# Loading, masks and hi/lo copies at the beginning of a hybrid encoder layer, rearranged

## The chip, the cores and the metric

The kernel runs on one core of a Trainium2 chip. Its engines are TensorE (PE; its weight loads are listed as PEld), VectorE (DVE), ScalarE (ACT), GpSimd (POOL) and SyncE (SP, which here only issues transfers). Each works through its own queue in order, and waits on semaphores for the others. The metric is the device time of one execution in microseconds (us).

## The reference

One layer of an encoder, 1024 tokens of width 1024, in float32:

```
u = rmsnorm(x, norm_mix_pre)
proj = u @ w_in                # columns: qa ka va ga | za (gate, 32) | qs ks vs
o_a = gated linear attention, both directions, from qa ka va za; then norm * silu(ga)
o_s = windowed attention (|i-j| <= 128) of 8 query and 2 key heads, with bias and sink
x = x + rmsnorm(concat(o_a, o_s) @ w_out, norm_mix_post)
x = x + rmsnorm(relu(rmsnorm(x, norm_mlp_pre) @ w_up)^2 @ w_down, norm_mlp_post)

rmsnorm(x, g) = x * rsqrt(mean(x*x) + 1e-6) * g
```

## The kernel before

Products are made of float32r parts: each operand is split into a hi part (a rounding copy) and a lo part (the rest, by a subtraction), and hi·hi, lo·hi and hi·lo are summed in PSUM. This is `dense_part`, 24 matmuls for 8 slices of the inner dimension.

The beginning is written out by the string `START`, one token a step. `x3` loads tile 3 of x (128 tokens, 512 KB) on SP's queue. `p3` (`norm_x`) makes u of that tile, transposed: ScalarE squares the tile with a sum per token (L292) and adds epsilon (L176); GpSimd raises to the power -1/2 (L181, called the power below); VectorE scales the tile by that and by the norm weights (`gb`, L294); TensorE transposes it in eight 128x128 blocks into two PSUM banks (`pxt`, L171); of each bank a hi copy goes to `uth` (by ScalarE, L93, or VectorE, L95) and then a lo copy to `utl` (VectorE, L302). `HALF_X` names the engine of each of the 16 hi copies, `a` for ScalarE and `v` for VectorE. There are two such banks in all, so a tile's transposes wait for the lo copies of the tile before.

`f` fetches a weight tile (512 KB, 128 columns of w_in) into `raw`; VectorE makes its hi part `wh`, GpSimd its lo part `wl` (L196). There are two `raw` buffers. `v01` is the v projection (vs) of tiles 0 and 1 from the first weight tile, `k02` the k projection (ks) of tiles 0 to 3 from the second, both into `pkv`; `k22`, `v11`, `v22` are the rest of both. `W` loads the gate's columns, `z02` and `z22` project them (`pz`), `gates`, `misc`, `bias` and `spread` set up small things. After `START` comes `gates(0)` with the first matmul into `pg`, and the long list `ORDER`.

`gb`, the norm weights in all 128 partitions, is made by `load_gb`: a 4 KB row is loaded, and two matmuls with a row of ones spread it over the partitions, from where VectorE copies it. `set_misc` builds `wdiag` and `mask_lt`, used later by the linear attention, on GpSimd.

Instructions stand in the program in this order, but a scheduler places them in the queue of each engine; the order of a queue is then fixed.

Of the kernel before, what the change touches and what calls it, by code (L numbers as in the profile page):

```python
# [13 lines left out]
F32 = mybir.dt.float32  # L14
# [3 lines left out]
ALU = mybir.AluOpType  # L18
# [38 lines left out]
 'pvo': 'lg'}  # L57

EVAC = {'vf': 'v', 'vt': 'v', 'kt': 'v', 'th': 'v'}
HALF_X = "avvvaavavvvvavvv"  # L60
W_HI = "vvaavv"
W_LO = "gggggg"

START = (
        "gb x0 x1 f p0 x2 x3 p1 p2 f v01 p3 W x4 x5 x6 x7 p4 p5 k02 gates p6 p7 bias k22 v11 z02 v22 f f misc "
        "z22 spread "
)

# [10 lines left out]
def hybrid_layer(tc, x, g_mix_pre, w_in, w_gu_f, b_g_f, w_gu_b, b_g_b, gla_norm, sink, rel_bias, w_out,  # L81
                 g_mix_post, g_mlp_pre, w_up, w_down, g_mlp_post, onehot, relmask, out):
    nc = tc.nc

    def Q(name):
        return getattr(nc, QUEUE[name])

    def E(c):
        return dict(v=nc.vector, g=nc.gpsimd)[c]

    def C(c, dst, src):
        if c == "a":
            nc.scalar.copy(dst, src)  # L93
        else:
            E(c).tensor_copy(dst, src)  # L95

    order = ORDER.split()
    with ExitStack() as ctx:
# [5 lines left out]
        def bank(tag, name="bk"):  # L104
            return ps.tile([128, 512], F32, tag=tag, bufs=BUFS[tag], name=name)

        def slot(tag, kb, dt, name, bufs=1):
            t = sb.tile([128, int(kb * KB)], dt, tag=tag, bufs=bufs, name=name)

            def cut(off, n, *shape):  # L110
                ap = t[:, int(round(off * KB)):int(round(off * KB)) + n]
                if len(shape) == 2:
                    ap = ap.rearrange("p (a b) -> p a b", a=shape[0])
                return ap

            def cut3(off, a, b):
                return cut(off, a * b, a, b)

            cut.three = cut3
            return cut  # L120
# [4 lines left out]
        wdiag = cst(0.5, 128)  # L125
        mask_t = sb.tile([128, 128], I32, name="mask_lt")
        mask_lt = mask_t[:, :]
        so = [1.0]

        def small(n):  # L130
            ap = cst(so[0], n)
            so[0] += n / KB
            assert so[0] <= 3.25 + 1e-9, so
            return ap
# [6 lines left out]
        dsc = small(32).rearrange("p (h n) -> p h n", h=4)  # L141
# [9 lines left out]
        def tiny(n=8, ring="misc"):  # L151
            r = rings[ring]
            r[1] += 1
            return r[0][r[1] % len(r[0])][:, 0:n]

        nc.scalar.preload_act_table_set("natural_log_exp_and_others")
        nc.gpsimd.memset(ident, 1.0)
        nc.gpsimd.affine_select(out=ident, in_=ident, pattern=[[1, 128]], base=0, channel_multiplier=-1,
                                compare_op=ALU.is_equal, fill=0.0)
        nc.vector.memset(mhalf, -0.5)  # L160
        nc.vector.memset(epsc, EPS)
        orow = wdiag[0:1]
        nc.vector.memset(orow, 1.0)
        nc.vector.memset(sgn[0:64, 0:1], 1.0 / 16)
        nc.vector.memset(sgn[64:128, 0:1], -1.0 / 16)
        nc.vector.memset(sgn[0:64, 1:2], -1.0 / 16)
# [61 lines left out]
            return p  # L228


        e0 = slot("G0", 16, F32, "e0")
        e1 = slot("G1", 16, F32, "e1")
        e2 = slot("G2", 16, F32, "e2")
        e2x = slot("GX", 4, F32, "e2x")
# [27 lines left out]
            return r  # L262


        gb = e0(12, 1024)
        xts = [e0(4 * t, 1024) for t in range(3)] + [s2(4 * t, 1024) for t in range(4)]
        xt = []

        def load_x(t):
            xt.append(xts[t % 7])  # L270
            nc.sync.dma_start(xt[t], x[0, t * 128:(t + 1) * 128, :])

        def load_gb():
            gr = e1(8, 1024)[0:1]
            nc.sync.dma_start(gr, g_mix_pre)
            for c in range(2):
                p = bank("ga", "pgb")
                nc.tensor.matmul(p, lhsT=orow, rhs=gr[:, c * 512:c * 512 + 512], start=True, stop=True)
                C("v", gb[:, c * 512:c * 512 + 512], p)

        zw = e4.three(0, 8, 64)

# [6 lines left out]
        def norm_x(t):  # L289
            xn = e1(4 * (t % 2), 1024)  # L290
            ss = tiny(1)
            nc.scalar.activation(xn, xt[t], AF.Square, scale=1.0 / 32, accum_out=ss)  # L292
            r = rstd_of(ss)
            nc.vector.scalar_tensor_tensor(out=xn, in0=xt[t], scalar=r, in1=gb, op0=ALU.mult, op1=ALU.mult)  # L294
            for k4 in range(2):
                p = bank("tr", "pxt")
                transpose4(p, [xn[:, (k4 * 4 + j) * 128:(k4 * 4 + j + 1) * 128] for j in range(4)])
                p3 = p.rearrange("p (a b) -> p a b", a=4)
                h_ = uth[t // 4][:, k4 * 4:k4 * 4 + 4, (t % 4) * 128:(t % 4 + 1) * 128]
                l_ = utl[t // 4][:, k4 * 4:k4 * 4 + 4, (t % 4) * 128:(t % 4 + 1) * 128]  # L300
                C(HALF_X[2 * t + k4], h_, p3)
                nc.vector.tensor_sub(l_, p3, h_)  # L302
# [5 lines left out]
        bias = s2.three(0, 8, 384)  # L308

        def set_misc():  # L310
            nc.gpsimd.memset(wdiag, 1.0)
            nc.gpsimd.affine_select(out=wdiag, in_=wdiag, pattern=[[1, 128]], base=0, channel_multiplier=-1,
                                    compare_op=ALU.not_equal, fill=2.0)
            nc.gpsimd.memset(mask_lt, 1)
            nc.gpsimd.affine_select(out=mask_lt, in_=mask_lt, pattern=[[1, 128]], base=0, channel_multiplier=-1,
                                    compare_op=ALU.is_gt, fill=0)
            nc.gpsimd.memset(dsc, 0.0)
            Q("misc").dma_start(gnh, gla_norm.rearrange("a p -> p a"))
            sk = tiny(8)
            Q("misc").dma_start(sk, sink.broadcast_to([128, 8]))  # L320
            nc.vector.tensor_scalar(nsink, sk, -1.0, None, op0=ALU.mult)
# [106 lines left out]
        for tok in START.split():  # L428
            k, a = tok[0], tok[1:]
            if k == "x":  # L430
                load_x(int(a))
            elif k == "p":
                norm_x(int(a))
            elif k in "zvk":
                q0, n = int(a[0]), int(a[1])
                if k == "z":
                    z_part(q0, n)
                else:
                    kv_part({"v": "vs", "k": "ks"}[k], q0, n)
            else:  # L440
                {"gb": load_gb, "W": load_zw, "f": fetch_next, "misc": set_misc, "gates": set_gates,
                 "bias": set_bias, "spread": spread_bias}[tok]()

        scm = e2(12.5, 264)
# [6 lines left out]
        W = W2.rearrange("p (c j) -> p c j", j=66)  # L451
# [640 lines left out]
        for q, (p, j) in enumerate(seq):  # L1092
# [32 lines left out]
            if (p, j) in ((1, NP - 1), (2, NP - 1)):  # L1125
                u0 = 4 * (p - 1)
                t = slot(("U2", "U3")[p - 1], 16, F32, "wd")
# [7 lines left out]
        for (r, c), tags in (((1, 0), ("S0", "G0")), ((1, 1), ("G1", "U0")), ((0, 1), ("U1",))):  # L1135
            for h, tag in enumerate(tags):
                t = slot(tag, 16, F32, "wd")
# [79 lines left out]
        for n, (i, u) in enumerate(steps):  # L1217
            p, _, _, banks = plan[i]
            sd, td = double(2 * n), double(2 * n + 1)
            for t in range(4):  # L1220
                for c in range(2):
                    for m, (a, b) in enumerate(((0, 0), (0, 1), (1, 0))):
                        nc.tensor.matmul(banks[t], lhsT=sd[a][:, c * 512 + t * 128:c * 512 + t * 128 + 128],  # L1223
                                         rhs=td[b][:, c * 512:c * 512 + 512],
                                         start=p in (1, 2, 3, 5) and u == 0 and c == 0 and m == 0,
                                         stop=u == 7 and c == 1 and m == 2, skip_group_check=True)
# [81 lines left out]
```

## Time and profile before

| | us |
|---|---|
| median of 3 runs | 1085.55 (1084.59 to 1087.48) |
| the profiled execution | 1088.56 |
| its span, first to last instruction | 1086.8 |
| TensorE busy | 1048.9 |
| VectorE busy | 744.0 |
| ScalarE busy | 525.5 |
| GpSimd busy | 161.4 |

Times in the trace count from the start of the span. The profiled execution's own time is 1.8 us above its span. Matmuls are pipelined, so TensorE's busy time includes some waiting inside it; the weight loads (PEld) show its pace.

### The profile page before, as it was taken

What the parts mean: (1) busy time and instruction counts of PE and PEld (TensorE: products, weight loads), DVE (VectorE), ACT (ScalarE), POOL (GpSimd) and SP (SyncE); (2) the same over time, 40 slices, a digit from 0 to 9 for tenths busy, and PEclk for the clock granted to TensorE, in tenths of its full rate; (3) what the DMA queues carried; (4) which work ended last, traced back from release to release, by engine and by line L of the source; (5) the groups of instructions that cost most, each with busy time, mean ns of one, the idle gap of its engine ahead of it and who ended that gap; (6) DMA issues with size and microseconds to landing.
All of it is one profiled execution on the core that took longest, in us unless ns stands there. A gap on an engine that the chain in (4) does not pass through costs nothing.

```text
span 1086.8 us, 13683 instructions
## 1 busy us (share of the span) xinstructions
PE 1048.9 (97%) x4950; PEld 858.0 (79%) x4950; DVE 744.0 (68%) x1165; ACT 525.5 (48%) x890; POOL 161.4 (15%) x246
## 2 busy tenths in 40 slices
PE   7999999999997999989999999999999999999996
PEld 5787788888885878768888888888778888888885
DVE  7659458799887767798665666564479764547564
ACT  5565324424766444466555555554444334345342
POOL 4211012111211111111221212112100000004002
PEclk9999999999998999999999999999999999999999
DMA  7355443613666432546563544537982333345522
GB/s 227 111 159 173 131 115 84 143 40 93 190 171 162 122 121 84 160 152 207 177 191 116 177 143 148 172 119 238 392 325 97 98 97 97 116 136 193 194 97 97
DMA packets 138805, 164.82 MB, mean 152 GB/s; under 512 B 17473, under 2 KB 94273, under 8 KB 138738
## 3 DMA queue, kind: packets, MB, share of 16 engines
q1 hardware_dynamic: 108626, 108.36, 32.2%
q0 software_dynamic: 22560, 37.76, 11.6%
q10 hardware_dynamic: 7552, 17.83, 5.1%
q8 instruction: 39, 0.64, 0.2%
q14 instruction: 28, 0.23, 0.1%
HBM read 111.47 MB, written 52.45 MB: 151 GB/s over the span
## 4 chain that ended last, share of the span: by engine, by line
PE 81%; DVE 9%; ACT 3%; issue 3%; DMA 3%; POOL 1%; SPq 0%; ACTq 0%; DVEq 0%; POOLq 0%
PE pa L994 16%; PE pa L1223 14%; PE pin L222 11%; PE pc L994 8%; PE pb L1223 6%; PE pc L1223 6%; PE pm L810 4%; PE pb L994 4%; PE pkv L222 2%; PE ppt L171 1%; PE pm L815 1%; PE pl L545 1%; DMA wd<-in_w_down_dram 1%; PE pkv L692 1%; PE pl L546 1%
## 5 line engine op out<-in xcount | busy, mean ns | idle before, releaser
L1223 PE MATMUL pa<-r 128*128 128x512 f32 x768 | 175.1, 389 | 0.8 <-DVE r L1163 0.8
L1223 PEld LDWEIGHTS pa<-r 128*128 128x128 f32 x768 | 144.0, 188 | 31.4 <-DVE r L1163 1.6
L1162 DVE TENSOR_TENSOR r<-ra,r 128x1024 fp32r<-128x1024 f32 x56 | 68.5, 1223 | 106.7 <-ACT r L1160 105.3
L1160 ACT CAST r<-ra 128x1024 fp32r<-128x1024 f32 x56 | 58.9, 1053 | 165.9 <-PE pa L1223 94.1
L994 PE MATMUL pa<-th,r 128*128 128x512 f32 x384 | 102.3, 389 | 0.7 <-ACT sn L1009 0.7
L994 PEld LDWEIGHTS pa<-th,r 128*128 128x128 f32 x384 | 72.0, 188 | 16.0 <-ACT sn L1009 1.1
L222 PE MATMUL pin<-uth,wh 128*128 128x512 f32 x256 | 70.9, 400 | 0.0
L1223 PE MATMUL pb<-r 128*128 128x512 f32 x288 | 69.7, 390 | 0.0
L222 PE MATMUL pin<-uth,wl 128*128 128x512 f32 x256 | 69.4, 396 | 0.0
L1223 PE MATMUL pc<-r 128*128 128x512 f32 x288 | 69.2, 389 | 0.0
L810 PE MATMUL pm<-wo,b 128*128 128x512 f32 x256 | 67.5, 403 | 1.5 <-ACT b L802 1.5
L222 PE MATMUL pin<-utl,wh 128*128 128x512 f32 x256 | 66.9, 392 | 0.0
L1163 DVE TENSOR_TENSOR r<-wd,r 128x1024 fp32r<-128x1024 f32 x52 | 63.4, 1219 | 3.8 <-ACT r L1161 3.8
L1223 PEld LDWEIGHTS pb<-r 128*128 128x128 f32 x288 | 53.9, 188 | 11.9 <-DVE r L1163 0.7
L1223 PEld LDWEIGHTS pc<-r 128*128 128x128 f32 x288 | 54.1, 188 | 11.2
L180 POOL TENSOR_SCALAR cst<-cst 128x1 f32<-128x1 f32 x16 | 12.1, 754 | 323.6 <-ACT wd L1185 288.7
L1068 DVE TENSOR_TENSOR r<-su,r 128x1024 fp32r<-128x1024 f32 x32 | 39.0, 1220 | 28.9 <-ACT r L1067 28.9
L1161 ACT CAST r<-wd 128x1024 fp32r<-128x1024 f32 x52 | 54.6, 1050 | 5.4 <-DMA wd<-in_w_down_dram 5.4
L810 PEld LDWEIGHTS pm<-wo,b 128*128 128x128 f32 x256 | 47.5, 192 | 11.3 <-ACT b L802 2.4
L222 PEld LDWEIGHTS pin<-utl,wh 128*128 128x128 f32 x256 | 47.8, 188 | 9.7
L1002 ACT ACTIVATE ar<-ar 128x512 f32<-128x512 f32 x42 | 26.6, 632 | 56.3 <-DVE ar L1013 56.3
L222 PEld LDWEIGHTS pin<-uth,wl 128*128 128x128 f32 x256 | 47.0, 188 | 8.4
(282 smaller groups left out, 2136.3 us busy)
## 6 DMA issues: line engine op xcount, KB each, us to landing
ra<-hss SPq DMA_DIRECT2D x32, 512.0 KB, 3.6
wd<-in_w_down_dram SPq DMA_DIRECT2D x28, 512.0 KB, 9.3
hss<-ar POOLq DMA_DIRECT2D x54, 256.0 KB, 5.0
ra<-hsx SPq DMA_DIRECT2D x24, 512.0 KB, 3.8
hsx<-ar POOLq DMA_DIRECT2D x47, 256.0 KB, 2.9
ra<-in_w_up_dram SPq DMA_DIRECT2D x16, 512.0 KB, 4.1
rb<-in_w_up_dram SPq DMA_DIRECT2D x16, 512.0 KB, 5.9
raw<-in_w_in_dram SPq DMA_DIRECT2D x14, 512.0 KB, 4.6
```

What stands on the lines that cost most here:

```text
L171: nc.tensor.transpose(dst_bank[:, i * 128:(i + 1) * 128], s, ident)
L180: nc.gpsimd.tensor_scalar(r, ss, more, EPS, op0=ALU.add, op1=ALU.add)
L222: nc.tensor.matmul(p[:, cs], lhsT=a[:, kt, :], rhs=b[:, kt, cs], start=k == 0, stop=k == 23)
L810: nc.tensor.matmul(pm[c], lhsT=OTH[:, kt, :], rhs=w_[kt][:, sl], start=(w_ is woh and kt == 0), stop=False)
L994: nc.tensor.matmul(ps_, lhsT=a[:, kt, :], rhs=b[:, kt, :], start=p in (1, 2, 5) and n == 0 and kt == 0, stop=n == 2 and kt == 3, skip_grou ...
L1002: nc.scalar.activation(x_, x_ if src is None else src, AF.Relu)
L1068: late.append(lambda: nc.vector.tensor_sub(d[1], src, d[0]))
L1160: nc.scalar.copy(sd[0], ra[n % 2])
L1161: nc.scalar.copy(td[0], src)
L1162: nc.vector.tensor_sub(sd[1], ra[n % 2], sd[0])
L1163: nc.vector.tensor_sub(td[1], src, td[0])
L1223: nc.tensor.matmul(banks[t], lhsT=sd[a][:, c * 512 + t * 128:c * 512 + t * 128 + 128], rhs=td[b][:, c * 512:c * 512 + 512], start=p in (1, ...
```

## The change

The token `gb` goes from `START`. x's tile 0 is loaded on ScalarE's queue, as that engine's first instruction. `gb` is loaded by one transfer on SP's queue that reads the 4 KB row for each of the 128 partitions (512 KB). `wdiag`, `mask_lt` and `dsc` are set at the program's beginning and not in `set_misc`. `HALF_X` gives 12 of the 16 hi copies to ScalarE, where it gave 5.

```diff
-HALF_X = "avvvaavavvvvavvv"
+HALF_X = "aaavaaavaaavaaav"
...
 START = (
-        "gb x0 x1 f p0 x2 x3 p1 p2 f v01 p3 W x4 x5 x6 x7 p4 p5 k02 gates p6 p7 bias k22 v11 z02 v22 f f misc "
+        "x0 x1 f p0 x2 x3 p1 p2 f v01 p3 W x4 x5 x6 x7 p4 p5 k02 gates p6 p7 bias k22 v11 z02 v22 f f misc "
...
+        e0 = slot("G0", 16, F32, "e0")
+        gb, x0 = e0(12, 1024), e0(0, 1024)
+        nc.scalar.dma_start(x0, x[0, 0:128, :])
         nc.scalar.preload_act_table_set("natural_log_exp_and_others")
+        nc.sync.dma_start(gb, g_mix_pre.broadcast_to([128, 1024]))
...
-        orow = wdiag[0:1]
-        nc.vector.memset(orow, 1.0)
+        nc.gpsimd.memset(wdiag, 1.0)
+        nc.gpsimd.affine_select(out=wdiag, in_=wdiag, pattern=[[1, 128]], base=0, channel_multiplier=-1,
+                                compare_op=ALU.not_equal, fill=2.0)
+        nc.gpsimd.memset(mask_lt, 1)
+        nc.gpsimd.affine_select(out=mask_lt, in_=mask_lt, pattern=[[1, 128]], base=0, channel_multiplier=-1,
+                                compare_op=ALU.is_gt, fill=0)
+        nc.gpsimd.memset(dsc, 0.0)
...
             xt.append(xts[t % 7])
-            nc.sync.dma_start(xt[t], x[0, t * 128:(t + 1) * 128, :])
-
-        def load_gb():
-            gr = e1(8, 1024)[0:1]
-            nc.sync.dma_start(gr, g_mix_pre)
-            for c in range(2):
-                p = bank("ga", "pgb")
-                nc.tensor.matmul(p, lhsT=orow, rhs=gr[:, c * 512:c * 512 + 512], start=True, stop=True)
-                C("v", gb[:, c * 512:c * 512 + 512], p)
+            if t:
+                nc.sync.dma_start(xt[t], x[0, t * 128:(t + 1) * 128, :])
...
         def set_misc():
-            nc.gpsimd.memset(wdiag, 1.0)
...
-            nc.gpsimd.memset(dsc, 0.0)
```

The scheduler's queues change with it. GpSimd's queue before, from the identity matrix on, in the program's beginning (`cst<-cst 128x1` is a power, of one x tile each; `wl_104` and `wl_166` are the lo parts of the first and the second weight tile; the selects write `ident`, `wdiag` and `mask_lt`):

```order
L158 AFFINE_SELECT cst_63<-cst_63 128x128
L181 TENSOR_TENSOR cst_63<-cst_63 128x1
L311 MEMSET cst_63 128x128
L314 MEMSET mask_lt_64 128x128
L312 AFFINE_SELECT cst_63<-cst_63 128x128
L181 TENSOR_TENSOR cst_63<-cst_63 128x1
L315 AFFINE_SELECT mask_lt_64<-mask_lt_64 128x128
L317 MEMSET cst_63 128x32
L452 MEMSET e2_81 128x1056
L196 TENSOR_TENSOR wl_104<-raw_101,wh_103 128x1024
L181 TENSOR_TENSOR cst_63<-cst_63 128x1 x2
L196 TENSOR_TENSOR wl_166<-raw_163,wh_165 128x1024
```

The same stretch of GpSimd's queue in the changed kernel, where the powers are L190 and the lo parts L205:

```order
L162 AFFINE_SELECT cst_63<-cst_63 128x128
L167 AFFINE_SELECT cst_63<-cst_63 128x128
L169 MEMSET mask_lt_64 128x128
L172 MEMSET cst_63 128x32
L205 TENSOR_TENSOR wl_104<-raw_101,wh_103 128x1024
L170 AFFINE_SELECT mask_lt_64<-mask_lt_64 128x128
L190 TENSOR_TENSOR cst_63<-cst_63 128x1 x2
L318 MEMSET e2_89 96x512
L445 MEMSET e2_89 128x1056
L205 TENSOR_TENSOR wl_166<-raw_163,wh_165 128x1024
L190 TENSOR_TENSOR cst_63<-cst_63 128x1 x4
```

The powers of tiles 0 and 1 stood ahead of `wl_104` and now stand behind it; those of tiles 2 and 3 stood ahead of `wl_166` and now stand behind it.

TensorE's queue before, from tile 1's second bank to the first matmuls of `k02` (`pkv_169` is the v projection, `pkv_256` the k projection; pxt 149 and 156 are tile 2's banks, 198 and 205 tile 3's):

```order
L171 MATMUL pxt_138<-cst_63,e1_80 128x128 x4
L222 MATMUL pkv_169<-uth_75,wh_103 128x256 x4
L171 MATMUL pxt_149<-cst_63,e1_80 128x128 x4
L222 MATMUL pkv_169<-uth_75,wh_103 128x256 x4
L222 MATMUL pkv_169<-uth_75,wl_104 128x256 x7
L171 MATMUL pxt_156<-cst_63,e1_80 128x128 x4
L222 MATMUL pkv_169<-uth_75,wl_104 128x256
L222 MATMUL pkv_169<-utl_76,wh_103 128x256 x8
L171 MATMUL pxt_198<-cst_63,e1_80 128x128 x4
L171 MATMUL pxt_205<-cst_63,e1_80 128x128 x4
L222 MATMUL pkv_256<-uth_75,wh_165 128x512 x8
```

And in the changed kernel:

```order
L180 MATMUL pxt_138<-cst_63,e1_88 128x128 x4
L231 MATMUL pkv_169<-uth_84,wh_103 128x256 x8
L231 MATMUL pkv_169<-uth_84,wl_104 128x256 x8
L231 MATMUL pkv_169<-utl_85,wh_103 128x256 x8
L180 MATMUL pxt_149<-cst_63,e1_88 128x128 x4
L180 MATMUL pxt_156<-cst_63,e1_88 128x128 x4
L180 MATMUL pxt_198<-cst_63,e1_88 128x128 x4
L180 MATMUL pxt_205<-cst_63,e1_88 128x128 x4
L231 MATMUL pkv_256<-uth_84,wh_165 128x512 x8
```

Tile 2's transposes stood between the matmuls of the v projection and now stand behind all 24 of them. From the first `pg` matmul on, the queues of all engines read the same as before.

## Rows read from the trace of the kernel before

**Rows 1.** The page: the chain that ended last, share of the span by engine.

```profile
PE 81%; DVE 9%; ACT 3%; issue 3%; DMA 3%; POOL 1%; SPq 0%; ACTq 0%; DVEq 0%; POOLq 0%
```

**Rows 2.** Windows: each engine's busy us (instructions), granted clock, DMA share, GB/s.

```profile
10.00:20.00 10.00, 7.84 (x36) 6.80 (x34) 9.62 (x12) 4.35 (x9) 7.15 (x7) 1.00 0.74 237
20.00:30.00 10.00, 9.63 (x59) 7.95 (x58) 9.52 (x14) 6.16 (x13) 1.65 (x3) 1.00 0.60 159
30.00:40.00 10.00, 9.99 (x61) 6.92 (x60) 9.74 (x15) 4.74 (x9) 2.15 (x2) 1.00 0.05 9
...
22.70:55.30 32.60, 32.58 (x169) 24.25 (x170) 22.35 (x34) 17.25 (x32) 7.50 (x7) 1.00 0.43 123
```

**Rows 3.** The chain in order of time, first 56 us: start, us, what.

```profile
8.90 0.98 POOL cst L181
11.11 2.33 POOL wl L196
13.44 0.52 POOL cst L181
13.98 1.28 DVE e L294
22.71 2.29 PE pkv L222 x9
55.70 0.23 PE pg L459
```

**Rows 4.** Timeline of the first 10 us: start, us, engine, instruction, idle before it.

```profile
1.21 0.84 SPq L271 DMA_DIRECT2D e<-in_x_dram  x2
3.86 0.45 SPq L203 DMA_DIRECT2D raw<-in_w_in_dram  x1
6.90 0.56 POOL L181 TENSOR_TENSOR cst<-cst 128x1 f32<-128x1 f32 x1 [5.11 <-ACT cst L176]
7.49 1.29 DVE L294 SCALAR_TENSOR_TENSOR e<-e,cst 128x1024 f32<-128x1024 f32 x1 [0.54 <-POOL cst L181]
8.69 0.78 DVE L95 CAST wh<-raw 128x1024 fp32r<-128x1024 f32 x1
8.83 1.57 PEld L171 LDWEIGHTS pxt<-cst,e 128*128 128x128 f32 x8 [4.18 <-DVE e L294]
9.85 0.29 POOL L315 TENSOR_SCALAR_AFFINE_SELECT mask_lt<-mask_lt 128x128 int32<-128x128 int32 x1
9.98 0.59 ACT L93 CAST uth<-pxt 128x512 fp32r<-128x512 f32 x1 [1.80 <-PE pxt L171]
```

**Rows 5.** Source L285: SP's wait for the first weight tile, from when.

```profile
L285 SPq EVENT_SEMAPHORE  x1: 17/17/17, 8.6 to 8.6; - x1
```

**Rows 6.** DMA issues: KB each, median us from issue to landing.

```profile
e<-in_x_dram SPq DMA_DIRECT2D x1, 512.0 KB, 4.1
raw<-in_w_in_dram SPq DMA_DIRECT2D x1, 512.0 KB, 9.0
wd<-in_norm_mlp_post_dram SPq DMA_DIRECT2D x1, 512.0 KB, 4.6
```

**Rows 7.** Window of 1 us, columns as in rows 2.

```profile
7.00:8.00 1.00, 0.00 (x0) 0.00 (x0) 0.51 (x1) 0.97 (x3) 1.00 (x4) 1.00 1.07 320
```

**Rows 8.** Timeline of TensorE's weight loads, 16 to 21 us.

```profile
16.69 0.98 PEld L222 LDWEIGHTS pkv<-uth,wh 128*128 128x128 f32 x4
20.10 1.04 PEld L222 LDWEIGHTS pkv<-utl,wh 128*128 128x128 f32 x8
```

**Rows 9.** Groups by form, first 60 us: busy us, mean ns of one.

```profile
L302 DVE TENSOR_TENSOR utl<-pxt,uth 128x512 fp32r<-128x512 f32 x16 | 10.7, 684 | 0.2
L95 DVE CAST uth<-pxt 128x512 fp32r<-128x512 f32 x11 | 7.3, 681 | 0.0
L95 DVE CAST wh<-raw 128x1024 fp32r<-128x1024 f32 x2 | 1.5, 732 | 0.0
L93 ACT CAST uth<-pxt 128x512 fp32r<-128x512 f32 x5 | 2.9, 587 | 5.9 <-PE pxt L171 5.8
```

More of the change, by code (lines that the diff above doesn't have):

```diff
@@ L228, in dense_half @@
             return p
-        e0 = slot("G0", 16, F32, "e0")
         e1 = slot("G1", 16, F32, "e1")
@@ L262, in dense @@
             return r
-        gb = e0(12, 1024)
         xts = [e0(4 * t, 1024) for t in range(3)] + [s2(4 * t, 1024) for t in range(4)]
@@ L310, in set_misc @@
         def set_misc():
-            nc.gpsimd.memset(wdiag, 1.0)
[L312 to L316, printed above, removed]
-            nc.gpsimd.memset(dsc, 0.0)
             Q("misc").dma_start(gnh, gla_norm.rearrange("a p -> p a"))
@@ L440, in hybrid_layer @@
             else:
-                {"gb": load_gb, "W": load_zw, "f": fetch_next, "misc": set_misc, "gates": set_gates,
+                {"W": load_zw, "f": fetch_next, "misc": set_misc, "gates": set_gates,
                  "bias": set_bias, "spread": spread_bias}[tok]()
```

## Prediction

> **What bounds the kernel now.** I first read the chain that ended last: TensorE holds 81% of it [rows 1]. So only what makes TensorE wait, or start later, can move the end. The change touches the beginning alone: from the first gate matmul (`pg`) on, every engine's instructions stand in the same order before and after. The question is therefore when TensorE reaches `pg`, and I went through the windows for that [rows 2]. TensorE is busy 7.84 of the 10 us from 10 to 20, 9.63 of the next 10, and without a gap from 22.7 us, where the k projection of the low half (`pkv` with the second weight tile, call it K1) begins, to 55.3 us: 32.58 busy of 32.60 us. From there on TensorE's work sets the pace, and `pg` comes about 33 us after K1 begins [rows 3]. So I ask one thing of the change: when does K1 begin? Before, at 22.71 us.
>
> Next, the chain in order of time, for what leads to 22.71 [rows 3]. It runs through GpSimd: the rstd power of x tile 1 (0.98), a memset, the lo part of the first weight tile (`wl`, 2.33), the power of x tile 2 (0.52), and only then VectorE's scaling of tile 2 at 13.98. GpSimd does its queue in order, and each power gates one x tile: scaling, transposes, hi and lo copies, projection. VectorE is nearly full beside it (9.62, 9.52 and 9.74 of 10 us from 10 to 40 [rows 2]), but the chain touches it only in short pieces.
>
> **The change part by part.**
>
> *Norm weights by a transfer.* Two TensorE broadcasts and two VectorE copies go. VectorE was through with them and idle for 0.54 us when the first power released it at 7.49 [rows 4], so removing them is worth nothing. In their place 512 KB run at the head of SP's queue, where 4 KB ran.
>
> *x's first tile on ScalarE's queue.* Its issue no longer waits behind SP's first, 0.4 us earlier than 1.21 [rows 4]. The first x tile landed at 5.3 us (1.21 + 4.1); the first weight tile, two transfers later, at 8.6, when SP passed its wait for it; the second weight tile, three later, at 12.9 (3.86 + 9.0) [rows 4 to 6]. So a 512 KB transfer takes 1.4 to 1.65 us of the shared flow. The weight tile is now behind one more of them and issued 0.4 us earlier: 8.6 + 1.4 − 0.4 = 9.6 us. Bounds: 8.2 if the tile on the other queue costs the first queue nothing; 10.3 if the replicated row is slower than a plain tile, as the later one of its shape was (4.6 us to landing against 4.1 for the first x tile [rows 6]). I take 9.6, because the DMA engines were fully busy in those microseconds (share 1.07 at 320 GB/s [rows 7]), which leaves a second queue nothing to add.
> The Trainium skill (DMA: Bandwidth & Descriptors, section "Issuing engines are not separate DMA queues") speaks against this part of the change: transfers begun on several engines run on the same 16 DMA engines and interleave, so only the issue time is saved. By it the tile lands at 9.6, without it at 8.2, and the sum below would be 1.4 us less.
>
> *Masks early.* Two memsets and a select stood between the powers of tiles 0 and 1, the other select behind them. All but the last move into GpSimd's first idle stretch (5.11 us before 6.90 [rows 4]). By itself that would bring the power of tile 1 forward by 1.4 us (8.90 − 7.46 [rows 3, 4]).
>
> *What GpSimd does instead.* This decides the forecast. In the new order `wl` of the first weight tile stands ahead of both first powers, with one mask select behind it. Before, it stood behind them. So the power of x tile 0, due at 6.90 us, now waits for a weight tile that lands at 9.6. Step by step: landing 9.6; VectorE's hi copy, 0.07 + 0.78 [rows 4]; `wl` 2.33 [rows 3]; select 0.29; power 0.56 [rows 4]: 13.6 us. The first scaling begins there and not at 7.49, 6.1 us later. ScalarE's squares, SP's later loads and GpSimd's queue all have slack here; VectorE and TensorE simply stand still.
>
> *From there to K1.* The two scalings take 1.29 each and end at 16.2. VectorE then has the hi copy of weight tile 2 (0.73) and the lo copy of tile 0's first half (0.68), which frees the first transpose bank at 17.6. The next lo copy, after one of half that size for the z weights (0.4, an estimate), frees the other at 18.7 [rows 4, 9]. Each four transposes take 0.8 at TensorE's pace of that time (1.57 for eight) and 0.35 to their reader (8.83 + 0.8 to 9.98) [rows 4], so tile 1's last hi copy, which stays on VectorE, ends at 20.5. Two more lo copies, and the scaling of tile 2 runs from 21.8 to 23.1. Meanwhile TensorE has the v projection of tiles 0 and 1, whose 24 matmuls now stand in one piece ahead of tile 2's transposes (before, those began behind the first 4). They start at 19.4, when ScalarE's copy of tile 1 is there.
> What one costs: the granted clock reads 1.00, the 2.4 GHz level, in all these windows [rows 2], yet the same weight loads took 0.245 us each before 20 us and 0.13 after [rows 8], as if at the lower level first. TensorE had worked in bursts from 8.83. It now starts 6 us later, so the pace may rise later too: 24 × 0.13, held up by the last hi copy, ends with the scaling at 23.1; 24 × 0.245 ends at 25.3. I take a value between, 24.0.
> The Trainium skill (TensorE: Matmul & The Clock Gate, "Part 1: The HAM clock gate") has the throttled state as the default, which activity releases. By it the slow price would hold for most of the piece, and K1 would come about 1.3 us later than in my sum. No row tells which of the two holds, since none shows a lower level here.
> Then tile 2 and tile 3 go through two banks: transposes 0.5 (four at 0.13), 0.35 to the reader, hi copy on ScalarE 0.59, lo copy 0.68, transposes 0.5, 0.35, hi copy 0.59 [rows 4, 8, 9]: 3.6 us. **K1 begins at 27.6 us instead of 22.71: +4.9.** Bounds: 23.1 + 3.6 less 1.4 with the tile at 8.2 gives 25.3 (+2.6); 25.3 + 3.6 plus 0.7 with it at 10.3 gives 29.6 (+6.9).
>
> *Hi copies to ScalarE.* Seven of eleven go from VectorE (0.681 each, 4.8 us) to ScalarE (0.587 each, 4.1 us) [rows 9]. ScalarE was busy 15.3 of the 30 us from 10 to 40 [rows 2] and can take them. Before K1, VectorE is late because of the powers, so the two saved there are already in the steps above. After K1 TensorE had no gap even with VectorE full, and can't be faster than its work. A few of its waits for a bank may come at tiles 6 and 7, between 0 and 0.7 us; I take 0.1. If that cover fails, VectorE has five copies, 3.4 us, fewer there to absorb it.
>
> **Sum.** 0 + 4.9 + 0.1 = +5.0 us at `pg`. All later work is issued relative to it, in the same order, so it reaches the end in full. The profiled execution has 1086.8 us of span and 1.8 around it, 1088.6; it becomes 1093.6. It was 3.0 above the median of the runs; on the median, 1085.55 + 5.0 = **1090.5 us**, 0.46% more.
>
> **Rivals.**
> *Nothing to measure:* the weight tile lands at 8.2 to 8.6, and TensorE's quick pace is there when the v projection starts: +2.6 to +3.2, 1088.4. For it: the quick pace was there at 20 us before [rows 8]. Against: the flow was full, and TensorE starts later.
> *Faster:* VectorE is the real bound of 10 to 40 us, as its busy time says, and `wl` isn't in the way. Then seven copies at 0.68 come off its path: 1085.55 − 4.8 = 1080.8. It needs the weight tile early enough for `wl` to end before the power is due, at 6.9: landing by 6.9 − 2.3 − 0.9 = 3.7. No 512 KB tile landed before 5.3, and this is the third on its queue. For smaller delays it decides from the point where `wl` costs less than 4.8 us on the path; I have it at 6.1.
> *Slower still:* reading one 4 KB row 128 times is much slower than any row shows, and the weight tile lands 2 us later than I say: +7, 1092.5.
>
> **How the numbers follow.** My forecast 0.66, nothing to measure 0.19, faster 0.06, slower still 0.09. One execution and the next differ by up to 0.3%, 3.3 us, which is also about what a measurement can tell. Of the forecast's own range of +2.6 to +6.9 a small part (0.03 of the 0.66) lies within that: slower 0.72, same 0.22, faster 0.06. The range goes from the lower case, with the runs' spread below it, 1086.8, to the slower one, 1093.0.
>
> **What would show it.** In the new trace: the hi copy of the first weight tile before any scaling; `wl` ending near 12.8; the first scaling near 13.6 (12.2 to 14.4); first transposes near 15.0 and not 8.83; K1 near 27.6; `pg` near 60.7; no TensorE gap between these two. If the first scaling stands before 10 us, the step on GpSimd's queue is wrong. If it stands at 13.6 and K1 before 25, the steps from there are. If `pg` is late by 5 and the end is not, some later wait gave it back.

## The result and the profile after

The changed kernel is slower: its runs stand at 1.0069 of the kernel before (95% interval 1.0056 to 1.0082), which is 7.5 us more; the medians are 1093.51 us and 1085.68. A second set of runs came to 1.0074 (1.0059 to 1.0089). The direction was forecast. The time was put at 1090.5 and at most 1093.0, so the median is 3.0 us above the forecast and 0.5 outside the range, and the rise is 7.5 us where 5.0 was forecast.

Its first profiled execution took 1090.4 us (span 1088.7), 3.1 below the median of its runs, while the one of before had lain 3.0 above its own. So the two spans say little here, and I read the start of the program in them, not the end. The page's chain looks like before [rows 1]:

```profile
PE 80%; DVE 7%; ACT 3%; DMA 2%; issue 2%; POOL 1%; ACTq 0%; SPq 0%; DVEq 0%; POOLq 0%
```

The windows of the changed kernel, columns as in [rows 2], the last from K1 to just ahead of `pg`:

```profile
10.00:20.00 10.00, 3.27 (x13) 2.48 (x14) 6.50 (x7) 3.27 (x7) 7.93 (x8) 1.00 0.93 313
20.00:30.00 10.00, 8.96 (x53) 7.73 (x53) 7.57 (x11) 5.62 (x12) 1.49 (x3) 1.00 0.48 122
30.00:40.00 10.00, 9.59 (x64) 8.13 (x63) 8.52 (x12) 7.59 (x15) 1.47 (x4) 1.00 0.01 2
28.00:61.40 33.40, 32.58 (x170) 24.50 (x171) 20.43 (x30) 19.24 (x37) 7.51 (x7) 1.00 0.30 89
```

TensorE works 3.27 us of the second ten where it worked 7.84. From K1 to `pg` it does the same 32.58 us of work as before, but over 33.40 us and not 32.60: after K1 there are now 0.8 us of gaps. The timeline of the changed kernel, 9 to 29 us, shows what it waited for:

```profile
9.43 0.69 DVE L95 CAST wh<-raw 128x1024 fp32r<-128x1024 f32 x1 [6.47 <-DMA raw<-in_w_in_dram]
10.21 2.34 POOL L205 TENSOR_TENSOR wl<-raw,wh 128x1024 fp32r<-128x1024 f32 x1 [8.27 <-DVE wh L95]
12.50 0.29 POOL L170 TENSOR_SCALAR_AFFINE_SELECT mask_lt<-mask_lt 128x128 int32<-128x128 int32 x1
12.76 1.07 POOL L190 TENSOR_TENSOR cst<-cst 128x1 f32<-128x1 f32 x2
...
13.35 2.48 DVE L294 SCALAR_TENSOR_TENSOR e<-e,cst 128x1024 f32<-128x1024 f32 x2 [3.23 <-POOL cst L190]
...
14.69 1.57 PEld L180 LDWEIGHTS pxt<-cst,e 128*128 128x128 f32 x8 [14.69 <-DVE e L294]
...
16.51 2.36 POOL L205 TENSOR_TENSOR wl<-raw,wh 128x1024 fp32r<-128x1024 f32 x1 [1.29 <-DVE wh L95]
...
17.07 2.08 DVE L287 TENSOR_TENSOR e<-raw,e 128x256 fp32r<-128x256 f32 x1
...
19.81 1.12 PE L180 MATMUL pxt<-cst,e 128*128 128x128 f32 x4 [1.49 <-DVE utl L302]
...
20.58 2.36 PE L231 MATMUL pkv<-uth,wh 128*128 128x256 f32 x8
...
28.03 1.20 PE L231 MATMUL pkv<-uth,wh 128*128 128x512 f32 x4
```

The reader sees the forecast chain: the weight tile lands (9.43), `wl` holds GpSimd, then come the two powers (12.76), and VectorE, idle for 3.23 us, scales at 13.35 where it scaled at 7.49 [rows 4]. The line that was not forecast is at 17.07: the lo half of the z weights, a quarter of a `wl` in size, takes VectorE 2.08 us. It begins while GpSimd's second `wl` runs (16.51 to 18.87) and ends just behind it. The lo copy that stands behind it in VectorE's queue is late by that, and tile 1's second four transposes, which need the bank that this copy frees, wait until 19.81. In the chain in order of time `pg` stands 6.05 us later than in [rows 3]:

```profile
61.75 0.23 PE pg L452
```

### The profile page after: what moved, and what is told of

It is laid out like the page before. It is cut to its first block, busy times and chain, and to the rows that moved or that the text cites. A ratio compares the mean times of both kernels' runs of the same rounds, so it can differ in the third digit from the quotient of the medians.

```text
span 1088.7 us, 13662 instructions
## 1 busy us (share of the span) xinstructions
PE 1043.9 (96%) x4946; PEld 855.9 (79%) x4946; DVE 739.2 (68%) x1155; ACT 528.3 (49%) x897; POOL 158.7 (15%) x246
## 4 chain that ended last, share of the span: by engine, by line
PE 80%; DVE 7%; ACT 3%; DMA 2%; issue 2%; POOL 1%; ACTq 0%; SPq 0%; DVEq 0%; POOLq 0%
PE pa L987 15%; PE pa L1216 14%; PE pin L231 12%; PE pc L987 8%; PE pb L1216 6%; PE pc L1216 6%; PE pm L803 4%; PE pb L987 3%; PE ppt L180 2%; DMA wd<-in_w_down_dram 1%; PE pm L808 1%; PE pkv L231 1%; PE pl L538 1%; PE pl L539 1%; PE pkv L685 1%
## 5 line engine op out<-in xcount | busy, mean ns | idle before, releaser
L1061 DVE TENSOR_TENSOR r<-su,r 128x1024 fp32r<-128x1024 f32 x32 | 39.1, 1221 | 28.6 <-ACT r L1060 28.6
```

Source lines behind the costliest of these rows:

```text
L1061: late.append(lambda: nc.vector.tensor_sub(d[1], src, d[0]))
```

## The experiments

Theory A: GpSimd's order delays the start, and the delay reaches the end. Rivals: B, the 512 KB of the replicated norm weights delay what is behind them; C, ScalarE's copies make it slow; P, TensorE's pace. A1 is the addition from the row at 17.07: VectorE stands still beside GpSimd's large subtractions. The table has times from each one's profile (us; `pg` is the start of its first matmul in the timeline, which lies 0.16 ahead of its row in the chain) and the ratio of its runs to those of the kernel before. Each edit makes the scheduler place the queues anew, so a version can differ from its parent in more than the lines shown, and no run changes TensorE's new order by itself. One profile's K1 is good to about 1 us: the two of before differ by 0.6, the two of the changed kernel by 1.1.

| kernel | first scaling | K1 | `pg` | K1 to `pg` | ratio (95%) |
|---|---|---|---|---|---|
| before | 7.49 | 22.71 | 55.54 | 32.8 | |
| e3 before, again | 7.23 | 22.09 | 54.76 | 32.7 | 1.0001 (0.9992–1.0011) |
| changed | 13.35 | 28.03 | 61.59 | 33.6 | 1.0069 (1.0056–1.0082) |
| e5 changed, again | 13.35 | 29.11 | 62.66 | 33.6 | 1.0074 (1.0059–1.0089) |
| e1 changed, x tile on sync | 6.62 | 22.95 | 56.56 | 33.6 | 1.0031 (1.0022–1.0040) |
| e2 before, x tile on ScalarE | 11.71 | 28.00 | 61.17 | 33.2 | 1.0051 (1.0039–1.0063) |
| e4 changed, tile asked for later | 10.14 | 25.45 | 59.45 | 34.0 | 1.0050 (1.0037–1.0063) |
| e6 changed, z lo on GpSimd | 13.45 | 25.99 | 59.52 | 33.5 | 1.0059 (1.0046–1.0072) |
| e7 before, norm weights by DMA | 8.86 | 23.94 | 56.62 | 32.7 | 1.0016 (1.0005–1.0026) |
| e8 before, new table | 7.32 | 23.00 | 56.49 | 33.5 | 1.0016 (1.0006–1.0027) |
| e9 changed, warm-up | 13.39 | 26.96 | 60.41 | 33.5 | 1.0064 (1.0048–1.0079) |
| e10 changed, lo on VectorE | 11.33 | 24.55 | 58.41 | 33.9 | 1.0031 (1.0019–1.0043) |
| e11 before, early masks | 7.33 | 23.50 | 56.25 | 32.8 | 0.9996 (0.9985–1.0007) |
| e12 e11 with warm-up | 7.34 | 24.65 | 57.77 | 33.1 | 1.0028 (1.0018–1.0039) |
| e13 e1 with lo on VectorE | 6.77 | 23.92 | 57.26 | 33.3 | 1.0040 (1.0025–1.0056) |
| e14 e8 with lo on VectorE | 7.20 | 22.76 | 56.24 | 33.5 | 1.0021 (1.0012–1.0030) |
| e15 before, lo on VectorE | 7.18 | 23.46 | 56.25 | 32.8 | 1.0011 (1.0003–1.0020) |

### The queue of x's first tile: undone, and done alone

e1, against the changed kernel (the tile then stands ahead of the norm weights' 512 KB on SP's queue):

```diff
-        nc.scalar.dma_start(x0, x[0, 0:128, :])
+        nc.sync.dma_start(x0, x[0, 0:128, :])
```

> The changed kernel with one part undone: x's first tile is loaded by the sync queue again, ahead of the norm weights; the replicating transfer, the early masks and the ScalarE copies stay. On GpSimd this puts the powers of tiles 0 and 1 ahead of `wl` of the first weight tile again. Theory A (GpSimd's order makes the change slow): first scaling near 7.5 to 8.5 us instead of 13.35, K1 near 23 to 24.5 instead of 28.03, `pg` 55.7 to 57.5 instead of 61.75, ratio to the kernel before 0.999 to 1.002. Rival B (the 512 KB of the replicated norm weights delay what is behind them): the first weight tile's hi copy stays at 9.4, K1 stays above 27 and the ratio at 1.005 or more. Rival C (ScalarE's copies and the order of TensorE behind them make it slow): first scaling early, but K1 above 26 and the ratio above 1.004.

e2, against the kernel before:

```diff
+        e0 = slot("G0", 16, F32, "e0")
+        nc.scalar.dma_start(e0(0, 1024), x[0, 0:128, :])
         nc.scalar.preload_act_table_set("natural_log_exp_and_others")
...
-            nc.sync.dma_start(xt[t], x[0, t * 128:(t + 1) * 128, :])
+            if t:
+                nc.sync.dma_start(xt[t], x[0, t * 128:(t + 1) * 128, :])
```

> The kernel before with one part of the change alone: x's first tile is issued by ScalarE ahead of its table load; the norm weights still come by one row and two matmuls, masks late, copies by VectorE mostly. GpSimd's order becomes `wl` of the first weight tile and then the powers of tiles 0 and 1. Theory A: hi copy near 8.6 to 9.0, `wl` to about 11.3, powers behind it, first scaling near 12 to 13 instead of 7.49, K1 3.5 to 5.5 later than 22.71, ratio 1.003 to 1.006. Rivals B and C (transfer of the norm weights, ScalarE's copies): neither is in this kernel, so the ratio is 0.999 to 1.001.

e2 alone makes the kernel before 5.5 us slower (0.51%), and nothing of the other three parts is in it. Its timeline:

```profile
8.82 2.34 POOL L198 TENSOR_TENSOR wl<-raw,wh 128x1024 fp32r<-128x1024 f32 x1 [7.04 <-DVE wh L95]
11.12 1.07 POOL L183 TENSOR_TENSOR cst<-cst 128x1 f32<-128x1 f32 x2
...
11.71 2.51 DVE L296 SCALAR_TENSOR_TENSOR e<-e,cst 128x1024 f32<-128x1024 f32 x2 [2.97 <-POOL cst L183]
```

Here x's tile is even there earlier (its square starts at 4.71 against 5.08 in e3), and yet the first scaling is 4.2 to 4.5 us later: it waits for a power, and `wl` now stands ahead of the powers. Theory A is shown for this part. e1 undoes it and gets back 4.1 of the 7.5 us; K1 is at 22.95, as early as A expected, but the ratio is 1.0031 and A had said at most 1.002. So A is not all of it.

e4 puts the powers first in another way, by asking for the weight tile later:

```diff
-        "x0 x1 f p0 x2 x3 p1 p2 f v01 p3 W x4 x5 x6 x7 p4 p5 k02 gates p6 p7 bias k22 v11 z02 v22 f f misc "
+        "x0 x1 p0 p1 f x2 x3 p2 f v01 p3 W x4 x5 x6 x7 p4 p5 k02 gates p6 p7 bias k22 v11 z02 v22 f f misc "
```

> The changed kernel with one token of the starting order moved: the first weight tile is asked for behind the norms of tiles 0 and 1 (x0 x1 p0 p1 f x2 ... instead of x0 x1 f p0 x2 x3 p1). The order of loads on the sync queue stays as it is; on GpSimd both powers then stand ahead of `wl`. x's first tile stays on ScalarE's queue. Theory A: first scaling at 8.5 to 10.5 us (VectorE's hi copies of the weight tile still stand ahead of it and end at 10.2), K1 24 to 26 instead of 28.03, ratio 1.001 to 1.004. Rivals B and C: K1 27 or later, ratio 1.005 or more.

K1 came as expected, the ratio (1.0050) above the 1.004 that A allowed. The timeline says why GpSimd's right order brought so little:

```profile
10.14 4.58 DVE L294 SCALAR_TENSOR_TENSOR e<-e,cst 128x1024 f32<-128x1024 f32 x2
10.46 3.18 POOL L205 TENSOR_TENSOR wl<-raw,wh 128x1024 fp32r<-128x1024 f32 x1
```

Two scalings take 4.58 us, not 2.48, and `wl` takes 3.18, not 2.34: each stood still while the other had its turn. The wait went from GpSimd's queue to this.

### The same kernels again

e3 is the kernel before and e5 the changed one, both without an edit.

> The kernel before, unchanged, for a second profile and as a measure of what the comparison gives for no change. Ratio 0.999 to 1.001. If the 3.4 us that the profiled execution of before lost to the other between 326 and 345 us (ScalarE's copy that waits for the output weights, granted clock 0.60 and 0.72 in two slices of 5 us) belong to the kernel, the second profile shows them again at the same place; if they are chance, it shows waits of w_out's landing below 4 us there, or at another place.

> The changed kernel, unchanged, for a second profile and more runs, since its first profile was its fastest run. Theory A, with its delay kept to the end: first scaling at 13.3, K1 at 28.0, `pg` 61.7 (0.8 either way), ratio 1.0056 to 1.0082 again. What is open is the difference between `pg` (6.05 later) and the runs (7.5): if the rest arises at a fixed place behind `pg`, this profile shows TensorE's lag behind the kernel before grow there; if it is chance, the lag moves up and down by 1 to 2 us at the places where it did so between the two profiles of before (80 to 100, 325 to 350, 460 to 490, 800 to 850 us).

For no change the comparison gives 1.0001. Up to the second transposes of tile 1 the two profiles of the changed kernel agree to 0.1 us; then e5 loses 1.1 us in the v projection:

```profile
20.57 2.35 PE L231 MATMUL pkv<-uth,wh 128*128 128x256 f32 x8
22.73 1.91 PE L231 MATMUL pkv<-uth,wl 128*128 128x256 f32 x8
24.43 1.50 PE L231 MATMUL pkv<-utl,wh 128*128 128x256 f32 x8
25.78 1.03 PE L180 MATMUL pxt<-cst,e 128*128 128x128 f32 x8
```

In the first profile the eight that begin at 22.73 took 1.17 us, here 1.91:

```profile
22.73 1.17 PE L231 MATMUL pkv<-uth,wl 128*128 128x256 f32 x8
```

The trace also holds a list of the clock levels granted to TensorE. Its first entry, the full clock, stands at 22.8 us in the first profile and at 25.3 in e5. So the same program finds TensorE at the quick pace about 2.5 us sooner or later: a share of P, by chance.

The rest lies behind `pg`. TensorE's lag behind e3, matmul by matmul from the end (us):

| at | before | changed | e5 | e2 | e1 | e6 |
|---|---|---|---|---|---|---|
| 60 | 0.8 | 6.9 | 7.9 | 6.4 | 1.8 | 4.8 |
| 320 | −0.1 | 6.1 | 7.9 | 5.3 | 1.7 | 4.8 |
| 350 | 1.4 | 4.1 | 7.6 | 4.3 | 2.4 | 4.9 |
| 500 | 1.7 | 4.2 | 8.5 | 5.4 | 3.4 | 4.8 |
| 850 to the end | 3.3 | 5.2 | 10.6 | 5.6 | 4.2 | 7.1 |

It moves up and down by 0.3 to 3 us at the same few places (80 to 100, 280 to 350, 460 to 490, 760 to 850 us) in kernels that are the same there, and even between two executions of one kernel. The first profile of the changed kernel got back 1.7 us there, the second lost 2.7. So no fixed later place gives back or adds to the delay, as far as these profiles tell. e3 has the same waits as before between 320 and 350 us, only shorter (ScalarE waits 6.8 us for the output weights there, 8.4 in before), so the waits belong to the kernel and their length changes from one execution to the next.

At 460 to 490 us TensorE's clock has a part in it. TensorE waits there, and the clock falls for a while in every profile. These are the windows of the changed kernel, first profile and e5:

```profile
455.00:490.00 35.00, 29.28 (x129) 23.83 (x129) 31.57 (x39) 22.41 (x35) 4.07 (x6) 0.95 0.44 137
455.00:490.00 35.00, 29.29 (x125) 23.84 (x124) 30.57 (x38) 21.73 (x37) 4.93 (x8) 0.90 0.44 142
```

Of the six kernels in the table, three have a mean of 0.95 (before, changed, e6), and their lag grows by at most 0.3 us from 350 to 500; three have 0.90 (e5, e2, e1), and it grows by 0.9 to 1.1. The mean alone does not decide it: e4 and e7 read 0.90 too, and their lag does not grow there.

### The lo half of the z weights

e6, against the changed kernel:

```diff
-            nc.vector.tensor_sub(zw[:, :, 32:64], zraw, zw[:, :, 0:32])
+            nc.gpsimd.tensor_sub(zw[:, :, 32:64], zraw, zw[:, :, 0:32])
```

> The changed kernel with one instruction moved: the lo half of the z weights (line 287, 2.08 us on VectorE at 17.07, while GpSimd's `wl` of the second weight tile runs from 16.51 to 18.87) is computed by GpSimd behind that `wl`. VectorE's order is otherwise the same. Theory A1 (VectorE's two-operand read of SBUF stood still until GpSimd's `wl` ended, and this held the second transpose bank): the transposes of tile 1's second half come at 17.7 to 18.4 instead of 19.81, the v projection 1 to 2 us earlier than 20.51, K1 at 26.0 to 27.3 instead of 28.03, `pg` 0.7 to 2 us earlier, ratio 1.004 to 1.0065. Rival (the 2.08 us lay beside a wait for something else, or TensorE's slow pace sets the time): tile 1's second transposes within 0.4 of 19.81 or K1 within 0.4 of 28.03, ratio 1.0055 to 1.008.

```profile
16.61 2.37 POOL L205 TENSOR_TENSOR wl<-raw,wh 128x1024 fp32r<-128x1024 f32 x1 [1.29 <-DVE wh L95]
...
17.30 1.97 PE L180 MATMUL pxt<-cst,e 128*128 128x128 f32 x8 [0.55 <-DVE utl L302]
...
18.94 0.73 POOL L287 TENSOR_TENSOR e<-raw,e 128x256 fp32r<-128x256 f32 x1
...
19.10 1.22 PE L231 MATMUL pkv<-uth,wh 128*128 128x256 f32 x4
```

With nothing else on VectorE moved, its second four transposes follow the first without a gap, the v projection starts at 19.10 instead of 20.6, and K1 is 2.0 (first profile) and 3.1 us (e5) earlier. A1 holds at the start. Of these gains 1.5 us are there when the v projection starts; the rest is how long that projection then takes (3.6 us, against 4.1 and 5.2), TensorE's pace. In the runs it is 1.1 to 1.6 us (1.0059 against 1.0069 and 1.0074), whose intervals overlap, and 1.0059 lies in the range expected of A1 and in that of its rival; so A1 is shown by the trace and not by the runs.

### The other three parts alone

e7, e8 and e11, each against the kernel before:

```diff
         def load_gb():
-            gr = e1(8, 1024)[0:1]
-            nc.sync.dma_start(gr, g_mix_pre)
...
+            nc.sync.dma_start(gb, g_mix_pre.broadcast_to([128, 1024]))
```

> The kernel before with one part of the change alone: the norm weights are replicated by the transfer (512 KB, sync queue, ahead of x's first tile) instead of one row, two matmuls and two copies. GpSimd's order stays. Rival B (the transfer delays what is behind it): the first weight tile's hi copy 0.7 to 1 us later than 8.9, and x's first tile later too, K1 0.8 to 2 us later, ratio 1.001 to 1.002. Theory A (only GpSimd's order matters): K1 within 0.6 us of 22.1 to 22.7, ratio 0.9992 to 1.0008.

```diff
-HALF_X = "avvvaavavvvvavvv"
+HALF_X = "aaavaaavaaavaaav"
```

> The kernel before with one part of the change alone: the new table of copies (ScalarE takes three in four of the transposed tiles). GpSimd's powers of tiles 0 and 1 stay ahead of the first `wl`, but the power of tile 3 falls behind the second `wl`. Theory A: first scaling near 7.3, first transposes near 8.7 as before; K1 from 0.5 earlier to 1.0 later, ratio 0.9995 to 1.0012. Rival C (ScalarE's copies make the change slow): K1 2 us later or more, ratio above 1.002.

```diff
+        nc.gpsimd.memset(wdiag, 1.0)
...
+        nc.gpsimd.memset(dsc, 0.0)
-        orow = wdiag[0:1]
...
+            orow = e1(12, 128)[0:1]
```

> The kernel before with one part of the change alone: the masks made ahead of everything else on GpSimd (the row of ones for the norm weights is then its own). Between the powers of tiles 0 and 1 one select of 1.1 us stays, two memsets and one select of 1.2 go. Theory: the first `wl` 0.4 to 0.8 us earlier than 10.5 to 11.1, K1 0 to 0.8 earlier than 22.1 to 22.7, ratio 0.9988 to 1.0003. Rival (the start's end is set elsewhere): K1 within 0.2, ratio 0.9995 to 1.0005.

B is a real share: 1.7 us (e7). In its timeline x's first tile, behind the 512 KB, is there at 6.71 and not at 5.08 to 5.34, and the first scaling follows at 8.86:

```profile
6.71 1.06 ACT L287 ACTIVATE e<-e 128x1024 f32<-128x1024 f32 x1 [3.05 <-DMA e<-in_x_dram]
...
8.86 1.28 DVE L289 SCALAR_TENSOR_TENSOR e<-e,cst 128x1024 f32<-128x1024 f32 x1 [5.75 <-POOL cst L181]
```

C is one too: 1.7 us (e8). Its K1, 0.3 to 0.9 us later than in before's two profiles, is in theory A's range, but its ratio of 1.0016 lies between what A (at most 1.0012) and rival C (above 1.002) had expected, so neither fits as it was put. K1 here is not the table's doing alone, either: the mean clock of the first 22 us is 0.92, as the list of levels has the lower one from 18.1 to 21.5 us.

```profile
0.00:22.00 22.00, 14.16 (x55) 10.48 (x56) 15.46 (x26) 12.05 (x22) 12.29 (x19) 0.92 0.77 249
```

The early masks are worth nothing that can be measured (e11): one select of 1.14 us still stands between the two powers. K1 was expected up to 0.8 us earlier and came 0.8 to 1.4 later, as the first weight tile was there only at 9.46 (8.7 at the latest in before's two) and its hi copy took 1.31 us; the runs show none of it. Alone the four parts come to 5.5 + 1.7 + 1.7 − 0.4 = 8.5 us, against 7.5 and 8.0 together.

### TensorE kept busy

e9 puts work on TensorE ahead of x's transposes, against the changed kernel (the bank that it writes is read by nobody); e12 does it with 8 in place of 60, against e11:

```diff
+        pw = bank("lg", "pwarm")
+        for i in range(60):
+            nc.tensor.transpose(pw[:, (i % 4) * 128:(i % 4 + 1) * 128], ident, ident)
```

> The changed kernel with 60 transposes of the identity ahead of x's first transposes, into a spare bank that nothing reads: work that is only there to keep TensorE busy in the 14.7 us in which it waits. Theory P (a share of the delay is TensorE's pace: the v projection's 24 matmuls took 4.0 us in one profile of the changed kernel and 5.7 in the other, against 3.1 at the quick pace of 0.13 each): x's first eight transposes take 1.0 to 1.2 us instead of 1.97, the v projection 3.1 to 3.4, K1 at 25.5 to 27 instead of 28.0 and 29.1, `pg` 59 to 60.5, ratio 1.004 to 1.006. Rival (VectorE's and GpSimd's chain sets the time, TensorE's pace is hidden behind it): K1 within 0.5 us of 28.0, ratio 1.0065 to 1.0085. If the pace stays slow through the 60, they end near 17 and the first transposes come 2 us later than 14.69.

> The same kernel with early masks and with 8 transposes of the identity in front of x's first, in the 2.4 us in which TensorE waits after the norm weights. Theory P: TensorE's quick pace (0.13 instead of 0.245 for a matmul of 256 columns) begins 1 to 3 us earlier than 20.1, K1 0.7 to 2 us earlier than in the kernel with early masks alone, ratio 0.997 to 0.9995. Rival (pace hidden): K1 within 0.3 of it. If the eight are slower than the wait is long, x's first transposes come up to 0.5 us later than 8.6 to 8.8.

The windows of e9:

```profile
5.00:10.00 5.00, 5.00 (x45) 4.84 (x44) 0.53 (x1) 2.67 (x6) 0.00 (x0) 1.00 1.05 361
10.00:15.00 5.00, 0.35 (x3) 0.27 (x3) 1.77 (x3) 0.00 (x0) 4.75 (x6) 1.00 0.90 244
15.00:20.00 5.00, 3.57 (x19) 2.94 (x18) 3.54 (x6) 3.84 (x8) 3.27 (x3) 0.55 1.01 393
20.00:25.00 5.00, 4.66 (x31) 4.39 (x29) 3.86 (x6) 1.65 (x5) 0.57 (x2) 0.77 0.46 101
```

The sixty were done at 10.1 us, and TensorE then waited 4.65 us for the first scaling. The granted clock fell to 0.55 in the window behind that wait, close to the lower level (1.2 GHz), and the eight transposes at 17.46 took 1.97 us, as without a warm-up. So P in the form "warm it early" failed: the v projection ran from 19.25 to 23.63, 4.4 us (without the warm-up 4.1, and 5.2 in e5, not the 5.7 of the expectation). K1 and `pg` fell into P's ranges, the ratio of 1.0064 just above, but by another cause: K1 was 1.1 us earlier than in the first profile, and in this kernel the lo half of the z weights had moved ahead of GpSimd's second `wl` (0.42 us at 16.39), which is the gain of e6; e6 without any warm-up is 1.0 earlier still. e12 came out slower than e11 and can't be used for P: with the eight in front, VectorE's scaling of tile 2 stands ahead of tile 0's last lo copy, and TensorE waits 3.02 us for that copy.

### Lo halves on VectorE

e10, against the changed kernel; e13 has the edit of e1 with it; e14 and e15 make it on the kernel before, with and without the new table:

```diff
-W_LO = "gggggg"
+W_LO = "vvgggg"
```

> The changed kernel with the lo halves of the first two weight tiles computed by VectorE instead of GpSimd: GpSimd then has the powers of tiles 0 and 1 ahead of everything large, and no `wl` runs beside VectorE's two-operand reads. VectorE does 2 x 1.3 us more. Theory A and A1: powers near 9 us, first scaling at 11.2 to 11.8 (behind VectorE's own hi and lo of the first weight tile) instead of 13.35, the z weights' lo half 0.4 us instead of 2.08, K1 at 25.5 to 27, `pg` 59 to 60.5, ratio 1.0035 to 1.006. Rival (VectorE is the bound of the start, and 2.6 us more on it cost what they save): K1 at 28 or later, ratio 1.007 or more.

> The changed kernel with two things undone or moved: x's first tile on the sync queue again, and the lo halves of the first two weight tiles by VectorE. No large subtraction of GpSimd runs beside VectorE's two-operand reads. If the rest of 3.3 us in the run with the tile on the sync queue was VectorE standing still (2.71 us instead of 1.28 for the scaling of tile 2), K1 is 0.5 to 2 us earlier than there and the ratio 1.000 to 1.002. If the replicating transfer keeps its 1.7 us, 1.001 to 1.0025. If it is something else: 1.003.

> The kernel before with the new table of copies (ScalarE three in four) and the lo halves of the first two weight tiles by VectorE. The new table alone cost 1.7 us, with the scaling of tile 2 at 2.71 us beside GpSimd's second `wl`. If that was the cause, the scalings take 1.28 each, K1 is at 20.5 to 22.5 and the ratio 0.998 to 1.0005. If ScalarE's copies themselves cost it: 1.001 to 1.002.

> The kernel before with the lo halves of the first two weight tiles by VectorE, nothing else. In the profile of before one scaling takes 2.53 us beside `wl` (1.25 more than the others) and the power of tile 2 waits for the first `wl`; against that stand 2 x 1.25 us more on VectorE, which is busy 4.7 to 4.9 of every 5 us there. Expected: 0.9985 to 1.0015; faster if standing still was on the path, slower if VectorE is the bound of the start.

e10 leaves x's tile on ScalarE's queue, where it is as late as in the changed kernel (6.36), and still wins 4.1 us, more than was expected: what GpSimd has ahead of the powers costs more than the queue itself. e13 asked whether the rest of e1 (3.4 us) was VectorE standing still. It didn't go (1.0040, which is 4.3 us; 3.1 without the 1.2 that e15 pays for the same lo halves), so that idea falls. What e1 has left of the change is B, C and the masks, alone 1.7 + 1.7 − 0.4 = 3.0 us; but its x tile is not behind the 512 KB as in e7, and its `pg` is only 1.4 us late, so how the 3.4 divide is not shown.

e14 has no scaling longer than 1.3 us and is still at 1.0021, where e15, the same without the table, is at 1.0011. So the table's price is 1.7 us with the lo halves on GpSimd (e8) and 1.1 with them on VectorE; the intervals of e14 and e15 overlap. From K1 to `pg`, with the same number of matmuls, it is 0.7 us in both pairs, so that part is not VectorE standing still but goes with ScalarE's copies. The groups by form of e14, first 60 us:

```profile
L302 DVE TENSOR_TENSOR utl<-pxt,uth 128x512 fp32r<-128x512 f32 x16 | 10.7, 687 | 1.6 <-ACT uth L93 1.5
L294 DVE SCALAR_TENSOR_TENSOR e<-e,cst 128x1024 f32<-128x1024 f32 x4 | 5.1, 1285 | 1.1 <-POOL cst L181 1.1
```

VectorE's lo copies had 0.2 us of idle time ahead of them [rows 9], now 1.6, of which 1.5 until ScalarE's hi copy was there (0.8 and 0.7 in e15): ScalarE does its copies behind its own squares. That this wait is the 0.7 us is argued, not shown; e2, with the old table, has 2.8 us of it. e15 is slower by 1.2 us, as if VectorE had no room there; no run shows that either. None of these versions is measurably faster than the kernel before.

## Where the prediction was right, and the step that failed

*Right: the mechanism, its place, and that it reaches the end.* The weight tile's hi copy was forecast for 9.7 and came at 9.43, the first scaling for 13.6 (13.35), the first transposes for 15.0 (14.69). That the delay is kept is seen in the table of kernels: each one's time in the runs, as a difference to before, lies within 1.5 below and 2.2 above its `pg` less the mean of before's two (55.15), 0.7 above on average over 15.

The Trainium skill (DMA: Bandwidth & Descriptors, "Issuing engines are not separate DMA queues") had the rule for the weight tile, that transfers begun on several engines interleave on the same DMA engines. The trace agrees: by it 9.6, without it 8.2, measured 9.43; and 9.64 in e1, where the tile is back on SP's queue, so the other queue bought the weight tile 0.2 us. It was worse than the forecast said: with the replicating transfer beside it, x's own first tile was there at 6.36 and not at 5.34.

*Wrong: two terms of the sum were too small, and a third is not one number.* The sum said +5.0 at `pg`; the two profiles of the changed kernel have +6.4 and +7.5 against the mean of before's two.

1. "after one of half that size for the z weights (0.4, an estimate)": it took 2.08 us. This is the step that failed. The instruction alone does take 0.41 us (before, at 21.55); what the step left out is `wl` running beside it on GpSimd. It put tile 1's second transposes at 19.81 and the v projection at 20.5, where the forecast had 19.4; in e6, without it, the v projection starts at 19.10. In e6's runs this is worth 1.1 to 1.6 us, not clear of their intervals; their median, 1092.39, would have been inside the range. The Trainium skill (SBUF — State Buffer, "SBUF: two separate sides") states the rule that I didn't apply: VectorE with two SBUF inputs and GpSimd reading SBUF share one pair of ports, whichever starts first holds it for its whole instruction, and the other stands still. The rows agree: the z half starts at 17.07 and ends 0.28 behind a `wl` that ran to 18.87; in e4 `wl` is the one that loses at first, 3.18 us.
2. The v projection, "24 × 0.13" to "24 × 0.245", taken as 4.6 us from start to end: 4.1 in the first profile, 5.2 in e5. The term was right within its bounds and in the mean, but it is not one number; with term 1 it put K1 at 28.0 and 29.1 instead of 27.6. The forecast said that no row tells which of the two prices holds; the list of clock levels does, its first entry standing at 20.1 us in before.
3. "between 0 and 0.7 us; I take 0.1" for the stretch from K1 to `pg`: every kernel with the new table has 33.3 to 34.0 us there, every one with the old table 32.7 to 33.2. It costs 0.7 in the pairs e8 to before and e14 to e15, the upper bound, and as a whole the table costs 1.1 to 1.7. I had reckoned its copies as a saving on VectorE before K1 and put no wait of VectorE's next instruction for them into the sum.

The trace of before already has a row of the kind that the first term left out, a scaling beside `wl` that took 2.53 us where the others of its shape took 1.27 to 1.30:

```profile
17.45 2.37 POOL L196 TENSOR_TENSOR wl<-raw,wh 128x1024 fp32r<-128x1024 f32 x1
18.37 2.53 DVE L294 SCALAR_TENSOR_TENSOR e<-s,cst,e 128x1024 f32<-128x1024 f32 x1
```

The profile that I counted from [rows 3] had `pg` 0.4 us later than the mean of before's two, which adds that much. Together 5.0, 1.0 for K1 (27.6 against 28.6 in the mean), 0.6 after it and 0.4 make 7.0, the mean `pg`. The last 0.5 to 1.0 us to the runs' 7.5 and 8.0 stay open; they are within the intervals. Two bounds of the forecast do not follow from their rows: 9.6 and the 0.5 us between the two transfers [rows 6] give 10.1 and not 10.3, and +6.9 gives 1092.5 and not 1093.0. The forecast itself hangs on neither. Nor does the early masks' gain stand in the sum, which was read as 1.4 us for the power of tile 1: e11 has that power at 8.75 us, before's two profiles at 8.90 and 8.64.

*The rivals.* "Nothing to measure" needed the tile at 8.2 to 8.6. "Faster" needed VectorE as the bound and `wl` out of the way; e1 and e13 have it out of the way and are still slower than before. "Slower still" came nearest in time (1092.5) by another cause than its own.

## What to carry to other kernels

Before moving a load to another queue, compare what stands in which order on every in-order engine: here one small power behind one large subtraction cost more than the whole move could win. When an instruction lands beside a GpSimd instruction of some us and reads two operands from SBUF on VectorE, price it at the end of the other one and not by its size. Moving copies to a less busy engine helps only if the next instruction in the chain does not then wait for that engine's queue.

## What the runs showed of the hardware

- The granted clock of a window can read 1.00 while TensorE goes at half pace: in both kernels it reads so from 0 us, and the v projection's weight loads took up to 0.245 us each at first and 0.13 later. The list of clock levels in the trace has no entry ahead of that change: its first stands at 20.1 us in before and at 22.8 and 25.3 in the changed kernel's profiles. A fall in the first 30 us is listed only where TensorE had been quick once and then waited: in e9 after 4.65 us (0.55 in the next window) and in e8 from 18.1 to 21.5.
- VectorE's scaling took 1.28 us alone, 2.71 beside a `wl` that had begun 0.7 us ahead of it (e1); GpSimd's `wl` took 2.34 alone and 3.18 when VectorE was first (e4).
- Two executions of the same kernel (before and e3) drift apart by 3.4 us between 320 us and the end, at a few places and not evenly.
